# A bank of two buffers for transposed keys, and a threshold search with two serial VectorE operations a bit

## The chip, the cores and the metric

The kernel runs on one core of a Trainium2 chip. The metric is the device time of one execution in microseconds; the time of a version is the median of its runs. One execution of each version is also recorded by the hardware profiler, and that recorded execution has a time of its own.

## The reference

One inference step of a one-layer hybrid encoder for a prompt of 1,024 tokens and eight samples of 16 tokens (128 more columns, 1,152 in all). What matters here is the sparse attention's choice of keys and the gated delta rule.

```python
h = _rmsnorm(x, norm_mix)
qa, ka, va, qi, ki, wi, qb, kb, vb, gb, bb, ab, ga, gbr = jnp.split(h @ w_in, ...)
...
# mixer A: every query keeps its top-k keys by an index score, then softmax attention on those
score = jnp.einsum('bqhs,bqh->bqs', jax.nn.relu(s), wi)
score = jnp.where(adm[None], score, NEG)
_, idx = lax.top_k(score, topk)
...
# mixer B: gated delta rule; q and k are l2-normalised, then a triangular system per chunk
qh = _l2norm(qb_c) * (DK ** -0.5)
kh = _l2norm(kb_c)
a_mat = strict_lower(kb @ kc.T * decay) + eye
sol = triangular_solve(a_mat, rhs)
...
x = x + (sigmoid(ga) * (oa @ w_proj_a) + sigmoid(gbr) * (ob @ w_proj_b)) @ w_out
x = x + (gelu(conv(h2 @ w_up_gate)) * (h2 @ w_up_val)) @ w_down
```

## The kernel before

Every dense product is made in three passes: weights and activations are split into a rounded part (H, wh) and a remainder (L, wl), and TensorE adds H·wh, L·wh and H·wl for each tile of 128 rows. The columns stand in three blocks of 384; one block of one tile of `w_in` is 8·3 = 24 products into one of three PSUM banks (`acc`). These products are the filler: they run from the start of the kernel until the feed-forward network takes over, and everything else of the mixers is set between them.

The program writes no fixed order. Each piece of work is a generator, a thread with a priority; at each `yield` it names the engine that it wants next, an event, a bank, or the end of its own transfers (`DMA`). `_Driver.run` (line 165) takes the thread that by the driver's own table of costs can start first, and among equals the one with the lowest number, and lets it issue its next instructions. So the order of instructions on each engine comes out of the driver's costs, and each engine then works through its list strictly in that order. A `_Banks` object (line 47) is a set of buffers that the driver knows of: a thread that yields the bank gets a buffer only once one has been given back, by the driver's clock. A tile that is taken straight from a pool (`p.tile`) is not known to the driver: the hardware waits for its last user, but the order is written as if there were no wait.

The stage at hand begins when the scores of the indexer are there, and runs beside the dense products. Two sets of threads share it.

The choice of keys (`topk_rows`, line 294) searches, for every query, the threshold that keeps the wanted number of scores, one bit at a time. Rows 0 to 2 (thread "v", priority 8) and row 6 ("s", priority 7) count on VectorE. Rows 3 to 5 ("a", priority 7, `ACT_SUM`) count on ScalarE: for each of 31 bits VectorE makes a candidate (`cand`, line 1344), ScalarE takes the sign of each score less the candidate and sums (three `ja` instructions of 768, 896 and 1,024 elements, line 1348), and VectorE compares (line 1351), scales the bit (line 1353) and puts it into the threshold (line 1355). All the small operations work on 128 x 3 elements of the tile `cola`. After the last bit VectorE turns the thresholds into masks (lines 1393 to 1422), with operations over whole rows of scores.

The delta rule's local part (`gdn_local`, line 1430) prepares four heads, 0 to 3. `gdn_squares` (line 1612) transposes queries and keys of a head in groups of 4, 4 and 1 tiles of 128 into a PSUM bank (`gd`, five of them); for keys, ScalarE copies the bank into the tile `kt` (line 1624) and SP stores it (line 1626); then ScalarE squares the bank in place and VectorE sums it and gives the bank back. `gdn_tiles` (line 1551) makes the 128 x 128 blocks `nt` and `at`; `gdn_rows` (line 1633) solves 72 small triangles of 16 x 16 on VectorE by 15 steps of two operations (`pr` and `zs`); `gdn_inverses` and `gdn_levels` (lines 1668 and 1688) join them to inverses of 64 x 64 by products, with ScalarE copies (`lv`, `W`) between them. `gdn_v` (line 1493) transposes the values through the same PSUM banks.

Beside this `evac_conv` (line 936) filters blocks of the projection in two buffers `ext`; it stores the last columns of each (`out_cb`, lines 986 and 987) in pieces of three elements.

`mixers` (line 660) runs `gdn_local` to its end, then waits for the three sets of thresholds (line 720), and only then spawns attention and the scan of the delta rule. At the end of attention the samples' outputs are stored, loaded again, split, and taken by the products with `w_proj_a`, which follow those with `w_proj_b`.

Of the kernel before, what the change touches and what calls it, by code (L numbers as in the profile page):

```python
# [7 lines left out]
F32 = mybir.dt.float32  # L8
F32R = mybir.dt.float32r
BF = mybir.dt.bfloat16  # L10
I32 = mybir.dt.int32
# [285 lines left out]
class _Kernel:  # L297
# [996 lines left out]
    def topk_rows(self, s0, s1, ACT_SUM, z):  # L1294
# [8 lines left out]
        def col(dt=F32):  # L1303
            o = next(free)
            return cols[:, o:o + nr] if dt == F32 else cols[:, o:o + nr].bitcast(dt)
# [31 lines left out]
        if ACT_SUM:  # L1337
            cand, bit = col(I32), col(I32)
            yield DVE
            nc.vector.scalar_tensor_tensor(ka[:, s], kk[:, s], 2.0, nn[:, s], op0=OP.mult, op1=OP.add)  # L1340
            nc.vector.memset(thr[:, s], 0)
            for b in range(30, -1, -1):
                yield DVE
                nc.vector.tensor_scalar(cand[:, s], thr[:, s], (1 << b) - (1 << 31), None, op0=OP.bitwise_or)
                for i in R:
                    o, n = segs[i][:2]
                    yield ACT
                    nc.scalar.activation(ja[:, :n], SC[:, o:o + n], AF.Sign, bias=cand.bitcast(F32)[:, i:i + 1],
                                         accum_out=cnt[:, i:i + 1])
                yield DVE  # L1350
                nc.vector.tensor_tensor(acc[:, s], cnt[:, s], ka[:, s], op=OP.is_ge)
                yield DVE
                nc.vector.tensor_scalar(bit[:, s], acc[:, s], float(1 << b), None, op0=OP.mult)
                yield DVE
                nc.vector.tensor_tensor(thr[:, s], thr[:, s], bit[:, s], op=OP.bitwise_or)
        else:
# [73 lines left out]
    def gdn_local(self, st):  # L1430
# [7 lines left out]
        self.kqs = _Banks(p, [128, 2, T], "kq", 2)  # L1438
        self.vcs = _Banks(p, [128, 512], "vc", 1)
        self.nts = _Banks(p, [128, 9, 128], "nt", 1)  # L1440
        self.lvs = _Banks(p, [128, 512], "lv", 2)
# [170 lines left out]
    def gdn_squares(self, kq, ss, w, gsc):  # L1612
        nc, p = self.nc, self.gd
        for a, z in GR:
# [6 lines left out]
            if w:  # L1621
                kt = p.tile([128, 512], F32, name="kt")
                yield ACT
                nc.scalar.copy(kt[:, :n * 128], pk[:, :n * 128])
                yield SP
                nc.sync.dma_start(gsc[:, a:z, 0], v3(kt, n))
            yield ACT
            nc.scalar.activation(pk[:, :n * 128], pk[:, :n * 128], AF.Square)
# [1439 lines left out]
```

## Time and profile before

| | |
|---|---|
| runs, us | 2136.8, 2140.67, 2141.2; median 2140.67 |
| the profiled execution's own time, us | 2142.78 |
| its span, first to last instruction, us | 2140.8 |
| mean granted TensorE clock | 0.984 |
| busy: PE, weight loads, DVE, ACT, POOL | 97%, 94%, 72%, 47%, 39% |
| instructions | 37,600 |

All instructions go through one helper (line 192), so the profile is read by tile names and by time. The search of the thread "a" stands between 256.7 us and 590.1 us (first and last `ja`), the key copies `kt` between 314.0 and 477.0 us. PE is TensorE, DVE VectorE, ACT ScalarE, POOL GpSimd; SP issues the transfers. "Idle before" in square brackets is the time in which the engine stood still ahead of an instruction, with what released it.

### The profile page before, as it was taken

How to read it: one execution, taken by the hardware profiler on the slowest of the kernel's cores; microseconds unless marked ns; L12 is line 12 of the kernel's file. 1: busy time of each engine (PE TensorE's matmuls, PEld its weight loads, DVE VectorE, ACT ScalarE, POOL GpSimd, SP SyncE). 2: the span in 40 equal slices, each digit the busy share in tenths (PEclk: the TensorE clock that was granted, in tenths of full speed). 3: DMA queues.
4: the chain of work that ended last, by engine and by line, in shares of the span. 5: the costliest groups of instructions: out<-in, count | busy, mean ns of one | idle time of the engine just before them, and what ended most of it. 6: DMA issues, size and time to landing. Idle time of an engine off the chain costs nothing.

```text
span 2140.8 us, 37600 instructions
## 1 busy us (share of the span) xinstructions
PE 2068.0 (97%) x13146; PEld 2007.1 (94%) x13146; DVE 1544.1 (72%) x3588; ACT 999.3 (47%) x1979; POOL 838.4 (39%) x1024
## 2 busy tenths in 40 slices
PE   7999998989999999999999999999999999999997
PEld 6899997979999999999999989999999999999997
DVE  7268988888756778784353778878788766857656
ACT  5267666665625566666223433333333344535333
POOL 5344434432234444554364445656556500201101
PEclk8999999989999999999999999999999999999998
DMA  5444366676556555546774433433444476656542
GB/s 196 110 132 101 84 184 158 161 192 180 160 167 210 179 179 159 160 130 217 246 230 146 131 69 65 81 84 64 83 66 81 89 181 212 191 175 215 179 140 92
DMA packets 318156, 314.56 MB, mean 147 GB/s; under 512 B 117436, under 2 KB 277008, under 8 KB 317840
## 3 DMA queue, kind: packets, MB, share of 16 engines
q1 hardware_dynamic: 317968, 312.17, 53.2%
q8 instruction: 104, 1.70, 0.4%
q14 instruction: 84, 0.69, 0.1%
HBM read 224.91 MB, written 88.81 MB: 147 GB/s over the span
## 4 chain that ended last, share of the span: by engine, by line
PE 53%; DMA 7%; DVE 3%; issue 1%; POOL 1%; ACT 1%; SPq 1%; DVEq 0%; ACTq 0%; POOLq 0%
PE up L192 22%; PE dn L192 14%; PE acc L192 10%; PE at L192 6%; DMA T<-in_w_down 1%; DMA evo<-gates 1%; SPq L192 1%; DMA pbT<-evo 1%; PE rp L192 1%; DMA obT<-sg 1%; DMA ppT<-evo 1%; DVE B L192 0%; POOL tg L192 0%; DMA x<-qkv 0%; DVE wl L192 0%
## 5 line engine op out<-in xcount | busy, mean ns | idle before, releaser
L192 PE MATMUL acc<-H,wh 128*128 128x384 f32 (+2 forms) x1344 | 478.8, 356 | 10.8 <-ACT wh L192 3.1
L192 PE MATMUL acc<-H,wl 128*128 128x384 f32 (+2 forms) x1344 | 458.9, 341 | 1.6 <-POOL wl L192 1.6
L192 PE MATMUL acc<-L,wh 128*128 128x384 f32 (+2 forms) x1344 | 458.6, 341 | 1.5 <-POOL L L192 1.3
L192 POOL TENSOR_TENSOR wl<-wr,wh 128x256 fp32r<-128x256 f32 (+1 forms) x288 | 232.3, 829 | 308.8 <-ACT wh L192 301.3
L192 PEld LDWEIGHTS acc<-H,wh 128*128 128x128 f32 (+1 forms) x1344 | 255.3, 190 | 21.8 <-ACT wh L192 5.1
L192 PEld LDWEIGHTS acc<-L,wh 128*128 128x128 f32 (+1 forms) x1344 | 255.5, 190 | 6.2 <-POOL L L192 2.0
L192 PEld LDWEIGHTS acc<-H,wl 128*128 128x128 f32 (+1 forms) x1344 | 254.9, 190 | 4.3 <-POOL wl L192 2.9
L192 POOL TENSOR_TENSOR ssq<-ssq,sqs 128x384 f32<-128x384 f32 x62 | 71.8, 1158 | 390.4 <-ACT sqs L192 385.2
L192 ACT CAST wh<-wr 128x1024 fp32r<-128x1024 f32 (+3 forms) x140 | 122.7, 883 | 149.5 <-PE dn L192 48.3
L192 POOL TENSOR_TENSOR wl<-s,wh 128x256 fp32r<-128x256 f32 x104 | 98.7, 968 | 146.6 <-ACT wh L192 146.6
L192 PE MATMUL up<-B,wh 128*128 128x288 f32 x704 | 142.2, 296 | 1.0 <-DVE u L192 1.0
L192 DVE SCALAR_TENSOR_TENSOR T<-fe,cwf,T 128x512 f32<-128x512 f32 x132 | 123.4, 935 | 17.8 <-ACT T L192 16.2
L192 PEld LDWEIGHTS up<-B,wh 128*128 128x128 f32 x704 | 112.9, 188 | 1.3 <-DVE u L192 1.3
L192 ACT ACTIVATE ja<-SC,cola 128x768 bf16<-128x768 f32 (+2 forms) x93 | 96.7, 1039 | 34.5 <-DVE cola L192 25.1
L192 ACT CAST wh<-s 128x512 fp32r<-128x512 f32 x88 | 52.5, 620 | 120.3 <-PE up L192 113.4
L192 PE MATMUL up<-T,wh 128*128 128x288 f32 x352 | 104.3, 296 | 1.8 <-DVE T L192 1.8
L192 PE MATMUL up<-B,wl 128*128 128x288 f32 x352 | 104.0, 296 | 0.0
L192 DVE TENSOR_TENSOR wl<-wr,wh 128x512 fp32r<-128x512 f32 (+1 forms) x87 | 71.8, 840 | 30.3 <-ACT wh L192 30.2
L192 POOL TENSOR_TENSOR cvc<-cvc,evo 128x384 f32<-128x384 f32 (+2 forms) x48 | 44.0, 917 | 76.8 <-ACT evo L192 53.7
L192 DVE TENSOR_SCALAR_CACHE_REDUCE e<-half,colv 128x384 bf16<-128x384 int16 (+5 forms) x96 | 71.1, 740 | 0.9
L192 PEld LDWEIGHTS up<-T,wh 128*128 128x128 f32 x352 | 66.4, 189 | 2.5 <-DVE T L192 2.5
L192 PE MATMUL acc<-MH,wl 128*128 128x384 f32 x192 | 65.3, 340 | 2.7 <-POOL wl L192 2.7
(507 smaller groups left out, 6108.0 us busy)
## 6 DMA issues: line engine op xcount, KB each, us to landing
wr<-in_w_in SPq DMA_DIRECT2D x48, 512.0 KB, 3.8
AT<-fv SPq DMA_DIRECT2D x22, 576.0 KB, 6.2
wr<-in_w_down SPq DMA_DIRECT2D x24, 512.0 KB, 3.6
T<-in_w_down SPq DMA_DIRECT2D x24, 512.0 KB, 3.6
wr<-in_w_up SPq DMA_DIRECT2D x22, 512.0 KB, 11.1
gates<-evo SPq DMA_DIRECT2D x48, 192.0 KB, 2.0
T<-AT SPq DMA_DIRECT2D x44, 192.0 KB, 3.7
qkv<-evo SPq DMA_DIRECT2D x36, 192.0 KB, 4.0
```

Source lines behind the costliest of these rows:

```text
L192: r = f(*a, **k)
```

## The change

The copies of transposed keys get a bank of two buffers that the driver knows of, in place of one tile from the pool. The candidate of the search carries the sign bit and the bit under test with it: while ScalarE counts, VectorE makes `base`, the candidate with the present bit taken out and the next one set; after the count one operation compares, and one shifts the result to its bit and joins it to `base`. The final threshold is the candidate without the sign bit.

```diff
         if ACT_SUM:
-            cand, bit = col(I32), col(I32)
+            cand, base, bit = col(I32), col(I32), col(I32)
             yield DVE
             nc.vector.scalar_tensor_tensor(ka[:, s], kk[:, s], 2.0, nn[:, s], op0=OP.mult, op1=OP.add)
-            nc.vector.memset(thr[:, s], 0)
+            nc.vector.memset(cand[:, s], 0)
+            nc.vector.tensor_scalar(cand[:, s], cand[:, s], (1 << 30) - (1 << 31), None, op0=OP.bitwise_or)
             for b in range(30, -1, -1):
+
                 yield DVE
-                nc.vector.tensor_scalar(cand[:, s], thr[:, s], (1 << b) - (1 << 31), None, op0=OP.bitwise_or)
+                nc.vector.tensor_scalar(base[:, s], cand[:, s], 3 << b - 1 if b else 1, None, op0=OP.bitwise_xor)
                 for i in R:
                     o, n = segs[i][:2]
                     yield ACT
                     nc.scalar.activation(ja[:, :n], SC[:, o:o + n], AF.Sign, bias=cand.bitcast(F32)[:, i:i + 1],
                                          accum_out=cnt[:, i:i + 1])
                 yield DVE
-                nc.vector.tensor_tensor(acc[:, s], cnt[:, s], ka[:, s], op=OP.is_ge)
+                nc.vector.tensor_tensor(bit[:, s], cnt[:, s], ka[:, s], op=OP.is_ge)
                 yield DVE
-                nc.vector.tensor_scalar(bit[:, s], acc[:, s], float(1 << b), None, op0=OP.mult)
-                yield DVE
-                nc.vector.tensor_tensor(thr[:, s], thr[:, s], bit[:, s], op=OP.bitwise_or)
+                nc.vector.scalar_tensor_tensor(cand[:, s], bit[:, s], b, base[:, s],
+                                               op0=OP.logical_shift_left, op1=OP.bitwise_or)
+            yield DVE
+            nc.vector.tensor_scalar(thr[:, s], cand[:, s], (1 << 31) - 1, None, op0=OP.bitwise_and)
...
         self.vcs = _Banks(p, [128, 512], "vc", 1)
+        self.kts = _Banks(p, [128, 512], "kt", 2)
...
             if w:
-                kt = p.tile([128, 512], F32, name="kt")
+                kt = yield self.kts
                 yield ACT
                 nc.scalar.copy(kt[:, :n * 128], pk[:, :n * 128])
                 yield SP
                 nc.sync.dma_start(gsc[:, a:z, 0], v3(kt, n))
+                self.drv.give(self.kts, kt)
```

Both edits change what the driver sees, so it writes another order on every engine from the middle of the indexer on. Three places matter for what follows. In the rows a wait on DMAHW0 to DMAHW7 is a wait for a transfer: SP's transfers take these eight lanes in turn, and a transfer's own row names the lane that it takes, which its predecessor on the lane must have left.

ACT, the key copies of head 1 (`kt`), with the counts of the search (`ja`), the weights (`wh`) and the filter (`ext`, `cvc`, `evo`) around them. Before:

```order
L192 COPY kt<-gd_3801 128x512 [waits DMAHW7_49,PE_49,Activation_49]
L192 ACTIVATE gd_3812<-gd_3812 128x128 [waits PE_49]
L192 ACTIVATE gd_3801<-gd_3801 128x512
L192 ACTIVATE ja,cola<-SC,cola 128x768 [waits DVE_49]
L192 ACTIVATE ja,cola<-SC,cola 128x896 [waits Activation_49]
L192 CAST wh<-wr 128x1024 [waits DMAHW6_49]
L192 ACTIVATE cvc_3868<-ext_3849,cwb 128x384 [waits DVE_49,Pool_49]
L192 COPY kt<-gd_3847 128x128 [waits DMAHW3_49,PE_49]
L192 ACTIVATE ja,cola<-SC,cola 128x1024 [waits Activation_49]
L192 ACTIVATE evo_3869<-ext_3849,cwb 128x384
L192 ACTIVATE ext_3904<-acc_3850 128x384 [waits DMAHW5_49,DMAHW4_49,PE_49]
```

ACT at the same place, with the change:

```order
L192 COPY kt_3799<-gd_3790 128x512 [waits PE_49]
L192 ACTIVATE evo_3708<-cvc_3677 128x384 [waits DVE_49]
L192 ACTIVATE gd_3792<-gd_3792 128x128 [waits PE_49]
L192 CAST wh<-wr 128x1024 [waits DMAHW4_49]
L192 ACTIVATE gm_3783<-gm_3783,ngc 128x128 [waits Pool_49]
L192 ACTIVATE gd_3790<-gd_3790 128x512
L192 ACTIVATE ja,cola<-SC,cola 128x768
L192 ACTIVATE ja,cola<-SC,cola 128x896 [waits Activation_49]
L192 ACTIVATE ja,cola<-SC,cola 128x1024 [waits Activation_49]
L192 ACTIVATE cvc_3890<-ext_3861,cwb 128x384 [waits DVE_49,Pool_49]
L192 COPY kt_3897<-gd_3886 128x128 [waits DMAHW1_49,PE_49]
L192 ACTIVATE ext_3920<-acc_3862 128x384 [waits DMAHW7_49,DMAHW0_49,PE_49]
```

The second copy no longer waits for a transfer; the third does, for the lane of the first buffer's store. The copy into `ext` waits for the small stores `out_cb` in both.

SP, the stores around the same copies. Before:

```order
L192 DMA gsc<-vc_3172 128x4x128 [waits DMAHW3_49,DVE_49]
L192 DMA out_cb<-ext_3387 128x3 [waits DMAHW4_49]
L192 DMA out_cb<-ext_3387 128x8x3 [waits DMAHW5_49]
L192 DMA wr<-in_w_in 128x1024 [waits DMAHW6_49,Pool_49]
L192 DMA gsc<-kt 128x4x128 [waits DMAHW7_49,Activation_49]
L192 DMA qkv<-evo_3624 128x384 [waits DMAHW0_49,DVE_49]
```

SP at the same place, with the change:

```order
L192 DMA gsc<-kt_3734 128x4x128 [waits DMAHW1_49,Activation_49]
L192 DMA kTs<-evo_3749 128x384 [waits DMAHW2_49,Activation_49]
L192 DMA out_kT<-evo_3749 128x384 [waits DMAHW3_49]
L192 DMA wr<-in_w_in 128x1024 [waits DMAHW4_49,Pool_49]
L192 DMA gm_3783<-gcr 128x128 [waits DMAHW5_49,DVE_49]
L192 DMA gsc<-vc_3088 128x4x128 [waits DMAHW6_49,DVE_49]
L192 DMA out_cb<-ext_3533 128x3 [waits DMAHW7_49]
L192 DMA out_cb<-ext_3533 128x8x3 [waits DMAHW0_49]
L192 DMA gsc<-kt_3799 128x4x128 [waits DMAHW1_49,Activation_49]
```

The first key store of this head and a load of weights have moved ahead of the two `out_cb`; the second key store stands behind them.

DVE, the last third of head 3's triangles (`pr`, `zs`). Before:

```order
L192 SCALAR_TENSOR_TENSOR pr<-ns,zs 72x100 [waits DVE_49]
L192 TENSOR_REDUCE zs<-pr 72x10 [waits DVE_49]
L192 SCALAR_TENSOR_TENSOR pr<-ns,zs 72x121 [waits DVE_49]
L192 TENSOR_REDUCE zs<-pr 72x11 [waits DVE_49]
L192 SCALAR_TENSOR_TENSOR pr<-ns,zs 72x144 [waits DVE_49]
L192 TENSOR_REDUCE zs<-pr 72x12 [waits DVE_49]
```

DVE at the same place, with the change:

```order
L192 SCALAR_TENSOR_TENSOR pr<-ns,zs 72x100 [waits DVE_49]
L192 SCALAR_TENSOR_TENSOR eq_6460<-SC,cola,eq_6460 128x896
L192 TENSOR_REDUCE zs<-pr 72x10 [waits DVE_49]
L192 TENSOR_TENSOR MB<-MB,eq_6460 128x896 [waits DVE_49]
L192 SCALAR_TENSOR_TENSOR pr<-ns,zs 72x121 [waits DVE_49]
L192 TENSOR_SCALAR MB<-MB 128x896 [waits DVE_49]
L192 TENSOR_REDUCE zs<-pr 72x11 [waits DVE_49]
L192 TENSOR_SCALAR MB<-SC,cola 128x1024
L192 SCALAR_TENSOR_TENSOR pr<-ns,zs 72x144 [waits DVE_49]
L192 TENSOR_SCALAR eq_6575<-MB 128x1024 [waits DVE_49]
L192 TENSOR_SCALAR MB,cola<-MB 128x1024 [waits DVE_49]
L192 TENSOR_REDUCE zs<-pr 72x12
```

The masks of the search (`MB`, `eq`) now stand between the steps of the triangles; before they followed them.

## Rows read from the trace of the kernel before

**Rows 1.** Page, part 1: busy time of each engine over the span
```profile
PE 2068.0 (97%) x13146; PEld 2007.1 (94%) x13146; DVE 1544.1 (72%) x3588; ACT 999.3 (47%) x1979; POOL 838.4 (39%) x1024
```
**Rows 2.** Stretches of 100 us: length, busy us by engine, granted clock, DMA, GB/s
```profile
300.00:400.00 100.00, 90.86 (x511) 85.94 (x509) 84.74 (x324) 64.63 (x142) 40.64 (x63) 0.97 0.70 183
400.00:500.00 100.00, 92.88 (x530) 88.09 (x529) 85.22 (x351) 58.62 (x126) 32.25 (x47) 0.90 0.71 185
```
**Rows 3.** Timeline of ACT: start, us, instruction, idle before it
```profile
341.99 1.06 ACT L192 ACTIVATE gd<-gd 128x512 f32<-128x512 f32 x2
352.91 0.58 ACT L192 COPY kt<-gd 128x512 f32<-128x512 f32 x1 [9.86 <-DMA gsc<-kt]
...
405.42 0.27 ACT L192 COPY kt<-gd 128x128 f32<-128x128 f32 x1 [2.80 <-DMA gsc<-kt]
```
**Rows 4.** The tile kt: all waits of its engine, us and times
```profile
  DMA gsc<-kt: 12.7, 2
```
**Rows 5.** Timeline of SP's issues around the wait
```profile
341.35 1.05 SPq L192 DMA_DIRECT2D out_cb<-ext  x2
342.50 0.61 SPq L192 DMA_DIRECT2D wr<-in_w_in  x1
343.21 0.38 SPq L192 DMA_DIRECT2D gsc<-kt  x1
```
**Rows 6.** The tensor out_cb: its 24 small stores, issue to landing
```profile
DMA to landing us min/median/max: 6.2/7.0/7.7
```
**Rows 7.** Timeline of DVE, the first operation after the wait
```profile
353.69 0.29 DVE L192 TENSOR_REDUCE ss<-gd 128x1 f32<-128x128 f32 x1 [6.81 <-ACT gd L192]
```
**Rows 8.** Timeline of PE: around the wait, and at 450 us
```profile
355.56 1.09 PE L192 MATMUL gd<-c,vc 128*128 128x128 f32 x4 [4.21 <-DVE at L192]
...
449.78 2.61 PE L192 MATMUL gd<-Z,lv 128*128 128x64 f32 x11 [1.07 <-ACT lv L192]
```
**Rows 9.** Three shorter stretches, columns as in rows 2
```profile
355.00:365.00 10.00, 9.44 (x41) 9.29 (x42) 9.96 (x36) 7.92 (x21) 6.57 (x12) 0.71 0.39 118
...
390.00:430.00 40.00, 40.00 (x230) 39.22 (x229) 33.90 (x138) 21.68 (x49) 14.72 (x25) 1.00 0.63 147
...
445.00:475.00 30.00, 25.08 (x158) 22.00 (x157) 22.70 (x93) 19.67 (x43) 9.98 (x13) 0.72 0.59 167
```
**Rows 10.** Timeline of PE: two products of an unbroken run of 15
```profile
299.71 0.34 PE L192 MATMUL acc<-L,wh 128*128 128x384 f32 x1
...
302.14 0.34 PE L192 MATMUL acc<-H,wh 128*128 128x384 f32 x1
```
**Rows 11.** Timeline of DVE: the four serial operations of a late bit
```profile
584.18 0.16 DVE L192 TENSOR_TENSOR cola<-cola 128x3 f32<-128x3 f32 x1
584.38 0.17 DVE L192 TENSOR_SCALAR cola<-cola 128x3 int32<-128x3 f32 x1
584.58 0.16 DVE L192 TENSOR_TENSOR cola<-cola 128x3 int32<-128x3 int32 x1
584.78 0.17 DVE L192 TENSOR_SCALAR cola<-cola 128x3 int32<-128x3 int32 x1
```
**Rows 12.** The tile cola on DVE: the one two-step operation of 128 x 3
```profile
L192 DVE SCALAR_TENSOR_TENSOR cola<-cola x1: 151/151/151, 254.1 to 254.1; 128x3 f32<-128x3 f32 x1
```
**Rows 13.** Timeline of ACT at 446 us: a late count and the copy behind it
```profile
446.00 0.93 ACT L192 ACTIVATE ja<-SC,cola 128x768 bf16<-128x768 f32 x1 [2.79 <-DVE cola L192]
...
449.38 0.62 ACT L192 COPY lv<-gd 128x256 f32<-128x256 f32 x2
```
**Rows 14.** Timeline of DVE: head 3's last triangle step, first and last masks
```profile
578.47 0.38 DVE L192 TENSOR_REDUCE zs<-pr 72x15 f32<-72x225 f32 x1
...
595.12 0.68 DVE L192 TENSOR_SCALAR MB<-SC,cola 128x768 bf16<-128x768 f32 x1
...
621.60 1.11 DVE L192 TENSOR_TENSOR MB<-MB,eq 128x1024 bf16<-128x1024 bf16 x1
```
**Rows 15.** Timeline of PE: the last products of attention
```profile
1018.82 1.05 PE L192 MATMUL at<-szn,svN 128*128 128x128 f32 x8
```
**Rows 16.** Timeline of POOL: the last piece of attention's output is split
```profile
1033.97 1.02 POOL L192 TENSOR_TENSOR L<-L,H 128x384 fp32r<-128x384 f32 x1 [2.80 <-ACT H L192]
```

## The prediction

> **What bounds the kernel now.** I read the busy shares first: TensorE is busy for 2068.0 of 2140.8 us [rows 1]. Nothing that another engine does can move the end unless it moves TensorE's work, its idle time, or its clock. The change adds and removes no product, so only the 73 us of idle time and the stretches at a lower clock are to be had. Stretch by stretch, the part in which the changed code runs holds more of both than the parts around it: 9.14 us of idle time between 300 and 400 us and 7.12 us between 400 and 500, with the granted clock at 0.97 and 0.90 [rows 2]. These 200 us are where the key copies and most of the search stand.
>
> The waits of the tile kt come next. ScalarE stood still for a key store twice, 12.7 us in all [rows 4]: 9.86 us ahead of the copy at 352.91, and 2.80 us ahead of the one at 405.42 [rows 3]. The first can be followed to TensorE. The store of the first buffer was issued at 343.21, behind two small stores issued from 341.35 [rows 5], which take 6.2 to 7.7 us to land [rows 6]. ScalarE's list is strictly in order, so the squares that stand behind the copy came late, VectorE's sums waited 6.81 us for them [rows 7], the PSUM banks came free late, and TensorE stood still for 4.21 us until 355.56 [rows 8]. It then came back at half speed: the mean granted clock from 355 to 365 us is 0.71 [rows 9], a mixture of 1.2 and 2.4 GHz. The second wait cost nothing: from 390 to 430 us TensorE was busy throughout [rows 9].
>
> **The key copies.** They stay twelve, with twelve stores, of the same size; the bank adds only memory. In the new order of head 1 the second copy waits for TensorE alone. The third waits for the first buffer's store, which now stands ahead of the two small stores, not behind them. So the 9.86 us go, and with them TensorE's 4.21 us. The clock goes with the gap: 9.44 busy us at 0.71 are 9.44 x 0.29 = 2.7 us lost. The bounds are nothing, if another wait takes the place, and 4.2 + 2.7 = 6.9. I take 6.9, because the row is this very wait and the order shows it gone. What is late next on ScalarE is the copy into the filter's buffer (ext), three instructions behind a count: it waits for the small stores, as before.
>
> **The search.** For each of 31 bits four serial operations become two, and one more (base) runs while ScalarE counts. Undisturbed, the steps of a bit are 0.20 us apart (584.18, 584.38, 584.58, 584.78) [rows 11], so two fewer save 0.4 us, and the search 31 x 0.4 = 12.4 us. Where VectorE is full the steps are further apart: of the 2.79 us that ScalarE waited for a candidate at 446.00 [rows 13] part was this. One operation joins two steps, a shift and an or; the only row for such an operation on 128 x 3 has 0.151 us, and the single-step ones 0.16 and 0.17 [rows 12, 11], so it costs no more. What is this worth on TensorE? Between 0 and the idle time that I can tie to a late candidate: at 449.38 ScalarE made a copy that stood behind three counts [rows 13], and TensorE had waited 1.07 us for it [rows 8]. I take that 1.1 and put the rest at nothing, since the cover is plain: while the search goes on TensorE has dense products to do, and these don't depend on it. If that cover went (no dense products left before the mixers end), the 12.4 us would count in full.
>
> Nor does the search alone open the next stage. Attention waits for the masks and for the delta rule's local part. Before, head 3's last triangle was done at 578.47 and the masks came after it, from 595.12 to 621.60 [rows 14]. In the new order these masks stand between the triangle's steps on VectorE, so head 3 is finished later, not earlier. Counting the dense products that stand ahead of attention's first product in TensorE's list gives 2,580 before and 2,694 now. An unbroken run of them has 14 steps from 299.71 to 302.14, 0.174 us each [rows 10], so attention is some 20 us of dense work later. That costs nothing by itself: 114 products done before need not be done after.
>
> **The sum.** 4.2 + 2.7 + 1.1 = 8.0 us. The profiled execution took 2142.8 us, so its like would be 2134.8; the median of the runs, 2140.67, stands 2.1 us lower. From the median the forecast is **2132.7 us**, 0.37% less.
>
> One rule speaks for a larger sum. The rows 300 to 500 us show TensorE idle for 9.14 + 7.12 = 16.3 us by its products, and for 14.06 + 11.91 = 26.0 us by its weight loads [rows 2]. The Trainium skill (Perfetto Trace Analysis, "Identifying the Most-Contended Engine") holds the products' busy share to be a poor measure and the weight loads' the good one. By it the most that the stretch can give would be 26.0 us instead of 16.3 before any clock; I go by the products, because my terms are single gaps between them.
>
> **Rivals.**
> First, **the wait only moves**. The copy into ext waits for the small stores themselves, and a second buffer doesn't change that. Between the second key copy and that copy the new list holds ScalarE work that I add up to some 7 us from like rows, against 6.2 to 7.7 us of landing [rows 6]; a microsecond or two of wait fits, 9.86 does not, unless SP issues late. The whole order is rewritten too, and such a collision can fall on another place. Then the 6.9 us stay and only 1.1 us go: 2139.6 us, no change. The key store issued at 343.21 freed ScalarE only at 352.9, after the small stores ahead of it [rows 3, 5]. The Trainium skill (DMA: Bandwidth & Descriptors, "Queues, rings and completion order") says that a transfer's signal lands only after all earlier writes of the same DMA engine. The trace agrees; by that rule every wait for a transfer issued behind an out_cb stays as long as it was.
>
> Second, **the pile after 445 us goes as well**. There head 0's levels meet head 3's keys and late counts of the search: 30.00 - 25.08 = 4.9 us idle, and 25.08 x 0.28 = 7.0 us of clock [rows 9], 11.9 in all, of which 1.1 is in my sum. If ScalarE, rid of late candidates, serves these levels in time, another 10.8 us go: 2121.9 us. Against it: the same pieces stand together in the new order, and the counts are packed closer.
>
> Third, on the other side, **the later attention runs into the products that need it**. By TensorE's list attention ended 282 dense products ahead of the first product with w_proj_a; now it is 99. From the last product of attention at 1018.82 [rows 15] the samples' outputs are stored, loaded and split until 1034.99 [rows 16]: 16.2 us. The new list leaves 99 products and 18 more ahead of the third block, 117 x 0.174 = 20.4 us. It fits by 4 us. If the store and the loads, which now meet the loads of gates and weights, took twice as long, 32.4 us, TensorE would stand still for 12.0 us and lose 2.7 us of clock after it: 2132.7 + 14.7 = 2147.4 us. The point from which it decides is a chain of some 26 us: 20.4, and the 5.3 that with 2.7 of clock eat up the 8.0 gained.
>
> **The numbers.** Forecast 0.50, for its mechanism is one row long and the order shows the wait gone; the wait moves 0.25; the pile goes too 0.10; late attention 0.15. A measurement of this kernel can tell about 0.2%, 4.3 us, from no change. Faster is then 0.50 + 0.10 = 0.60, same 0.25, slower 0.15. The range has to reach the second rival's 2121.9 below and, for what of the third is short of its price, nearly 2147.4 above: 2121 to 2146. The forecast's own range is 2127 to 2136, from half of the key term on the one side to half of the pile on the other.
>
> **What would show it.** Right: no wait of ScalarE for gsc<-kt above 3 us; no gap of TensorE near 4 us while heads 0 to 2 are prepared; idle time between 300 and 500 us near 11 us in place of 16.3; the search's last count some 12 us earlier, near 578 us; the masks among head 3's triangles, and attention's first product later than before. Wrong: a wait of ScalarE for out_cb of 5 us or more, with the same gap behind it; a clock as low as 0.90 between 400 and 500 us with new gaps ahead of it; or TensorE idle for over 5 us at the first products with w_proj_a.

## The result, and the profile after

The changed kernel takes 2125.01 us, the median of four runs (2120.38 to 2129.47), beside 2138.76 us for the kernel before (four runs, 2136.8 to 2141.2). The ratio is 0.9934, with a 95% interval of 0.9914 to 0.9955. The time lies in the range of 2121 to 2146 us and on the side that was forecast, but the gain is 13.7 us where 8.0 were worked out. The profiled execution took 2129.47 us, its span 2127.7.

The page of the changed kernel, part 1, stands against [rows 1]:

```profile
PE 2058.5 (97%) x13146; PEld 2000.3 (94%) x13146; DVE 1532.1 (72%) x3556; ACT 1003.4 (47%) x1984; POOL 838.4 (39%) x1022
```

Its stretches, with the columns of [rows 2]; the third answers to the last of [rows 9]:

```profile
300.00:400.00 100.00, 96.95 (x560) 94.50 (x559) 91.22 (x365) 75.11 (x161) 42.15 (x64) 0.98 0.74 191
400.00:500.00 100.00, 97.99 (x610) 94.11 (x609) 92.58 (x365) 68.91 (x144) 35.76 (x51) 0.97 0.81 188
445.00:475.00 30.00, 30.00 (x203) 27.72 (x202) 27.26 (x93) 20.75 (x48) 10.22 (x13) 0.91 0.90 176
...
900.00:1000.00 100.00, 95.55 (x604) 91.88 (x603) 66.85 (x201) 65.89 (x156) 51.21 (x78) 0.95 0.65 203
```

The gain comes out of the 200 us that the prediction named. TensorE's idle time there fell from 16.3 us to 3.05 + 2.01 = 5.1. What the clock takes (busy time times what the granted clock lacks to 1) fell from 90.86 x 0.03 + 92.88 x 0.10 = 12.0 us to 96.95 x 0.02 + 97.99 x 0.03 = 4.9. From 445 to 475 us there is no idle time in place of 4.9 us. That stretch no longer holds the whole pile, though: the first product of the levels (`gd<-Z,lv`) starts at 439.0 us in place of 449.8. From 430 to 475 us 2.0 us of idle time are left of 7.1 (the rows stand under e). A part is given back between 900 and 1000 us, where attention now stands: 4.45 us idle, against 2.11 before, at a clock of 0.95 in place of 1.00.

TensorE's waits from 300 to 500 us (engine and tile, what it waited for, us in total, times, longest):

```profile
PE gd L192 <- DMA vc<-qkv: 2.0, 1, 2.0
PE gd L192 <- ACT lv L192: 1.2, 1, 1.2
PE acc L192 <- ACT ext L192: 1.0, 1, 1.0
```

The largest is for a load of values (`vc`), which before was none of its waits. ScalarE's two waits for key stores [rows 3, 4] are gone; what is left of its waits in the same range, 230 to 700 us, for `kt` and for the small stores:

```profile
ACT kt L192 <- PE gd L192: 2.1, 2, 1.5
ACT ext L192 <- DMA out_cb<-ext: 1.4, 2, 0.9
```

The search ends 43 us earlier. First the counts on ScalarE (first and last start in us; before, the last was at 589.0), then two steps of a late bit on VectorE, with work on masks (`MB`) between them:

```profile
L192 ACT ACTIVATE ja<-SC,cola x93: 915/1042/1153, 261.4 to 546.2; 128x768 bf16<-128x768 f32 x31, 128x896 bf16<-128x896 f32 x31, 128x1024 bf16<-128x1024 f32 x31
```

```profile
543.10 0.15 DVE L192 TENSOR_TENSOR cola<-cola 128x3 int32<-128x3 f32 x1
543.22 0.29 DVE L192 TENSOR_SCALAR MB<-MB 128x512 bf16<-128x512 bf16 x1
543.43 0.16 DVE L192 SCALAR_TENSOR_TENSOR cola<-cola 128x3 int32<-128x3 int32 x1
...
587.21 0.38 DVE L192 TENSOR_REDUCE zs<-pr 72x15 f32<-72x225 f32 x1
```

The joined operation takes 0.16 us, as was taken from [rows 11, 12]. Head 3's last triangle step starts at 587.21, 8.7 us later than in [rows 14], and attention's last products start later too, against 1018.82 in [rows 15]:

```profile
1043.74 1.05 PE L192 MATMUL at<-szn,svN 128*128 128x128 f32 x8
```

### The profile page after: what moved, and what is told of

Its sections match the earlier page's. It is cut to its first block, busy times and chain, and to the rows that moved or that the text cites. A ratio compares the mean times of both kernels' runs of the same rounds, so it can differ in the third digit from the quotient of the medians.

```text
span 2127.7 us, 37559 instructions
## 1 busy us (share of the span) xinstructions
PE 2058.5 (97%) x13146; PEld 2000.3 (94%) x13146; DVE 1532.1 (72%) x3556; ACT 1003.4 (47%) x1984; POOL 838.4 (39%) x1022
## 4 chain that ended last, share of the span: by engine, by line
PE 79%; DVE 8%; DMA 6%; ACT 2%; issue 2%; POOL 2%; SPq 1%; DVEq 0%; POOLq 0%; ACTq 0%
PE acc L192 29%; PE up L192 22%; PE dn L192 15%; PE at L192 7%; PE gd L192 2%; PE ix L192 1%; DVE e L192 1%; SPq L192 1%; DMA qr<-qiT 1%; POOL wl L192 1%; PE ac L192 1%; DMA wr<-in_w_in 1%; PE rp L192 1%; DMA T<-in_w_down 1%; DVE B L192 1%
## 5 line engine op out<-in xcount | busy, mean ns | idle before, releaser
L192 ACT ACTIVATE z<-z,mx 128x896 f32<-128x896 f32 (+7 forms) x83 | 63.2, 766 | 20.1 <-DVE mx L192 19.7
```

What stands on the lines that cost most here:

```text
L192: r = f(*a, **k)
```

## The experiments

Three things changed together: a second key buffer, two serial operations in place of four, and the lists that the driver writes. The runs take them apart. They ran in three groups, each on a chip of its own with the kernel before beside it: a to d (median of the kernel before 2134.6 us), e, g, n1 and m1 (2135.0 us), and the rest (2132.7 us). So across groups only ratios and gains are compared, not times. The ratio stands as recorded, with its interval; it can differ from that of the two medians by some 0.001 (n2: 0.9960 and 0.9972). "Idle" is TensorE's from 300 to 500 us, "clock" what the granted clock takes there (as above, but from one row for the whole 200 us, whose clock is rounded to 0.01, some 2 us), both from the one profiled execution; "last count" is the last start of `ja`. "Changed" is the execution of the section above.

| run | lists | operations a bit | key buffers | median, us | ratio to before (95%) | idle, us | clock, us | last count, us |
|---|---|---|---|---|---|---|---|---|
| before | before's | 4 | 1 | | 1 | 16.3 | 12.9 | 589.0 |
| a | before's | 4 | 2 | 2132.22 | 0.9990 (0.9973 to 1.0006) | 13.6 | 9.3 | 583.3 |
| b | before's | 2 | 1 | 2131.81 | 0.9989 (0.9974 to 1.0005) | 14.2 | 9.3 | 581.4 |
| e | before's | 2 | 2 | 2128.99 | 0.9975 (0.9959 to 0.9991) | 12.6 | 5.6 | 575.8 |
| g | changed | 4 | 2 | 2130.44 | 0.9980 (0.9970 to 0.9991) | 9.0 | 3.8 | 547.9 |
| d | changed | 2 | 1 | 2124.52 | 0.9958 (0.9943 to 0.9973) | 10.6 | 0.0 | 545.2 |
| changed | changed | 2 | 2 | 2125.01 | 0.9934 (0.9914 to 0.9955) | 5.1 | 5.8 | 546.2 |
| after again | changed | 2 | 2 | 2120.34 | 0.9933 (0.9916 to 0.9950) | 4.1 | 2.0 | 537.5 |
| c | own, old work and bank | 4 | 2 | 2137.38 | 1.0019 (1.0005 to 1.0033) | 14.0 | 7.4 | 587.3 |
| n1 | own, old work | 4 | 1 | 2151.20 | 1.0075 (1.0053 to 1.0097) | 28.5 | 17.2 | 613.2 |
| n2 | own, old work | 4 | 1 | 2126.73 | 0.9960 (0.9944 to 0.9976) | 15.5 | 12.9 | 590.4 |
| h | own, one yield a bit | 4 | 1 | 2135.28 | 1.0010 (0.9996 to 1.0023) | 16.0 | 11.0 | 520.9 |
| m1 | own, new work | 2 | 2 | 2121.82 | 0.9940 (0.9920 to 0.9959) | 11.1 | 1.9 | 551.2 |
| p | own, new work, packed stores | 2 | 2 | 2118.59 | 0.9926 (0.9911 to 0.9941) | 7.6 | 5.8 | 561.6 |

### a: the second buffer alone, every list as before

```diff
-                kt = p.tile([128, 512], F32, name="kt")
+                kt = p.tile([128, 512], F32, name="kt", bufs=2)
```

> Only the second buffer: the tile kt gets two buffers in its pool, of which the planning driver knows nothing, so every instruction of every engine stands in the order of before. Theory 1 (the key store's wait held TensorE): ScalarE's 9.86 us wait ahead of the second key copy of head 1 is gone, TensorE's 4.2 us gap near 355 us and the half clock after it go with it, about 6.9 us less than before, near 2132 us. Rival A (the rewritten order gave the gain): the wait only moves to the copy into ext, 0 to 3 us less. Rival B (the shorter search gave the gain): as rival A.

The wait for the key store is gone (12.7 us before [rows 4], 0.4 now), and yet the ratio is 0.9990, not told from 1. The gap stayed at its place. TensorE's timeline, SP's issues ahead of it, and the stretch that answers to the first of [rows 9]:

```profile
354.26 0.63 PE L192 MATMUL gd<-c,vc 128*128 128x128 f32 x4 [3.33 <-DMA vc<-qkv]
```

```profile
341.28 1.06 SPq L192 DMA_DIRECT2D out_cb<-ext  x2
342.44 0.57 SPq L192 DMA_DIRECT2D wr<-in_w_in  x1
343.11 0.38 SPq L192 DMA_DIRECT2D gsc<-kt  x1
343.58 0.46 SPq L192 DMA_DIRECT2D qkv<-evo  x1
344.13 0.64 SPq L192 DMA_DIRECT2D gm<-gcr  x1
344.87 0.40 SPq L192 DMA_DIRECT2D vc<-qkv  x1
```

```profile
355.00:365.00 10.00, 10.00 (x50) 9.82 (x49) 6.64 (x34) 5.51 (x14) 5.45 (x9) 0.83 0.78 223
```

Before, TensorE stood still for 4.21 us ahead of the very same product, the first with this load of `vc`, and the trace put it down to VectorE [rows 8]. With that out of the way it stands still for 3.33 us, for the load of the values, which was issued 3.6 us behind the two small stores `out_cb`; the clock after it is 0.83 in place of 0.71. ScalarE, too, has a new wait there: 3.10 us at 350.92, for the load of weights (`wr`) issued at 342.44. The transfers of 340 to 350 us, rate in 40 slices of 0.25 us:

```profile
GB/s 289 362 363 375 369 350 246 205 291 289 249 34 18 18 122 16 0 16 16 0 16 0 0 16 16 33 262 82 16 49 33 49 33 98 82 98 82 16 334 285
DMA packets 2265, 1.31 MB, mean 131 GB/s; under 512 B 1249, under 2 KB 2159, under 8 KB 2265
```

From 342.75 to 349.5 us the rate is 0 to 122 GB/s but for one slice of 262, with 205 to 375 ahead of it and 285 to 334 behind it; 1,249 of the packets are under 512 bytes, and the two `out_cb` alone have 1,152 pieces. So the first rival's mechanism was at work: what is issued behind the small stores comes late, and whoever waits for it waits on. The Trainium skill (DMA: Bandwidth & Descriptors, "Specifications") names 512 bytes as the least transfer for full rate; the pieces of `out_cb` have 12. The trace agrees, as far as it goes: the rate is low while they are under way. No run here tries pieces near 512 bytes.

### b: the short search alone, every list as before

```diff
-                nc.vector.tensor_scalar(cand[:, s], thr[:, s], (1 << b) - (1 << 31), None, op0=OP.bitwise_or)
+                raw.tensor_scalar(base[:, s], cand[:, s], 3 << b - 1 if b else 1, None, op0=OP.bitwise_xor)
+                note(DVE, 0.08)
...
-                nc.vector.tensor_scalar(bit[:, s], acc[:, s], float(1 << b), None, op0=OP.mult)
+                raw.scalar_tensor_tensor(cand[:, s], bit[:, s], b, base[:, s],
+                                         op0=OP.logical_shift_left, op1=OP.bitwise_or)
+                note(DVE, 0.08)
                 yield DVE
-                nc.vector.tensor_tensor(thr[:, s], thr[:, s], bit[:, s], op=OP.bitwise_or)
+                note(DVE, 0.08, True)
```

> Only the search with two serial operations a bit, in the order of before: the driver is told of the four old operations at their old places, so what is left out is one VectorE operation a bit and two steps of each candidate's chain. One key buffer. Theory 1: 0 to 2 us less than before (the 1.1 us of the copy that stood behind three counts), near 2138 us; ScalarE's 25.1 us of waiting for candidates falls by half or more. Rival A: no change within 2 us. Rival B: 8 us less or more, 2131 us or below.

Here `raw` issues an operation that the driver does not see, and `note` tells it the cost of one that is not issued. 0.9989, and again not told from 1. The waits for key stores stay (12.9 us), TensorE waits 2.56 us at 353.76 for the same load of values. ScalarE's waits for candidates (`cola`) fell from 25.1 us to 10.9, as expected, and the time hardly moved. The gap of 1.07 us that the prediction tied to a late candidate is gone, but the wait just ahead of it, for a load (`W`), grew from 0.91 to 2.30 us. In before's lists each edit measures some 2 us, and by the intervals at most some 6.

### e: both edits, every list as before

The edits of a and b together.

> Both edits in the hardware, the second buffer and the two serial operations, but every engine keeps the list of before: the driver is told of the old four operations and of no bank. If the edits act by themselves (theory 1, the forecast's terms), their parts add up: TensorE's 4.2 us gap of before at 355 us and the lower clock go, and late candidates no longer hold ScalarE, 2132.7 us by the forecast's sum, a ratio near 0.996. If the two edits alone hide under each other's waits (each alone gave 0.999), the ratio is 0.998 to 0.999, 2130 to 2133 us on this chip's scale of 2134.6. If the gain of the change needs the new list (theory 2), this stays 7 us or more above the 2124 to 2125 us of the changed kernel.

0.9975: within the intervals the two parts add up, 2135.0 x 0.0025 = 5.3 us, in place of 8.0. The wait for the values is still there, 3.69 us at 351.42. The changed kernel's interval (0.9916 to 0.9950, third group) does not touch this one, so the lists carry some of the gain. One place where they do is the largest gap of the pile after 445 us. Before, TensorE waited 2.43 us there for a copy `lv`; ScalarE's rows between its two copies (some left out) hold no count and no wait:

```profile
457.58 0.73 ACT L192 COPY lv<-gd 32x256 f32<-32x256 f32 x2
458.34 1.05 ACT L192 CAST wh<-wr 128x1024 fp32r<-128x1024 f32 x1
...
461.50 0.73 ACT L192 COPY lv<-gd 32x256 f32<-32x256 f32 x2
```

```profile
462.28 0.68 PE L192 MATMUL gd<-Z,lv 128*64 128x64 f32 x8 [2.43 <-ACT lv L192]
```

It is the order of ScalarE's list that makes this gap: it is 2.43 us in a, b and e as well. In the changed kernel's list the four copies of this step stand together:

```profile
445.89 1.50 ACT L192 COPY lv<-gd 32x256 f32<-32x256 f32 x4
```

There the gap is gone in the changed kernel's first profile, 0.24 us in its second and 0.92 us in d and g (below). The stretch from 430 to 475 us, which holds the pile in all of them: of the kernel before, of e, of g with its four operations in the changed lists, and of the changed kernel:

```profile
430.00:475.00 45.00, 37.88 (x219) 34.09 (x218) 37.60 (x152) 29.71 (x63) 15.66 (x21) 0.77 0.71 195
```

```profile
430.00:475.00 45.00, 39.86 (x269) 37.30 (x268) 41.38 (x172) 29.11 (x64) 14.50 (x18) 0.92 0.80 208
```

```profile
430.00:475.00 45.00, 42.21 (x297) 39.34 (x296) 42.56 (x178) 33.34 (x73) 13.90 (x19) 1.00 0.80 182
```

```profile
430.00:475.00 45.00, 42.99 (x287) 39.84 (x286) 42.19 (x166) 30.33 (x69) 12.73 (x16) 0.92 0.81 173
```

### c and d: one edit with its own lists

c has the three lines on the bank of the change and the old search; d has the new search and one buffer from the pool, and its lists are the changed kernel's, row for row.

> The change without its search: a bank of two key buffers that the driver knows of, the old search of four operations. The driver writes an order of its own. Theory 1: no wait of ScalarE for a key store above 3 us, about 7 us less than before, near 2132 us, give or take what the other order does. Rival A: anything between 2124 and 2147 us, with no relation to the waits of kt. Rival B: no change, within 3 us of before.

> The change without its bank: the short search as changed, one key buffer from the pool. Its order of instructions is that of the changed kernel, row for row, so against the changed kernel it differs only by the waits on the one buffer. Theory 1: the third copies, whose predecessor's store stands behind the small stores out_cb, wait up to 8 us in head 1; 3 to 7 us slower than the changed kernel, 2128 to 2132 us, and only 7 to 11 us faster than before. Rival A: within 3 us of the changed kernel, near 2126 us. Rival B: as rival A.

The bank with the lists that the driver then writes makes nothing faster (1.0019). The new search with its lists gives 0.9958 without a second buffer. What the buffer is worth there shows in d's ScalarE and TensorE timelines:

```profile
465.26 0.27 ACT L192 COPY kt<-gd 128x128 f32<-128x128 f32 x1 [9.27 <-DMA gsc<-kt]
```

```profile
467.10 0.45 PE L192 MATMUL acc<-H,wh 128*128 128x384 f32 x1 [1.63 <-ACT evo L192]
474.95 0.44 PE L192 MATMUL acc<-H,wh 128*128 128x384 f32 x1 [1.69 <-ACT wh L192]
```

The stretch from 450 to 500 us, first of d, then of the changed kernel's second profile ("after again"):

```profile
450.00:500.00 50.00, 44.73 (x262) 42.58 (x260) 41.14 (x159) 29.59 (x58) 14.82 (x21) 1.00 0.72 172
```

```profile
450.00:500.00 50.00, 49.41 (x302) 47.66 (x300) 47.23 (x189) 33.66 (x68) 16.99 (x24) 1.00 0.78 196
```

With one buffer the last key copy waits 9.27 us, and TensorE is idle for 5.3 us there in place of 0.6. The ratios differ by about as much, 0.0025 x 2133 = 5.3 us, but the gains by the medians only by 2.3 us (10.1 and 12.4), and the intervals overlap (0.9943 to 0.9973 and 0.9916 to 0.9950). By the trace the buffer pays, at 465 us in the new lists, not at 353 in the old; the times make that likely and do not show it.

### g: four operations in the changed kernel's lists; and the changed kernel again

```diff
-                nc.vector.tensor_scalar(base[:, s], cand[:, s], 3 << b - 1 if b else 1, None, op0=OP.bitwise_xor)
+                raw.tensor_scalar(cand[:, s], thr[:, s], (1 << b) - (1 << 31), None, op0=OP.bitwise_or)
+                told("tensor_scalar", base[:, s], cand[:, s])
...
-                nc.vector.scalar_tensor_tensor(cand[:, s], bit[:, s], b, base[:, s],
-                                               op0=OP.logical_shift_left, op1=OP.bitwise_or)
+                raw.tensor_scalar(bit[:, s], acc[:, s], float(1 << b), None, op0=OP.mult)
+                raw.tensor_tensor(thr[:, s], thr[:, s], bit[:, s], op=OP.bitwise_or)
+                told("scalar_tensor_tensor", cand[:, s], bit[:, s], b, base[:, s])
```

> The lists of the changed kernel on TensorE, ScalarE, GpSimd and SP, row for row, with two key buffers, but the old search in them: four serial operations a bit, and the driver is told of the new ones. With the runs before it this fills the square of old and new lists by four and two operations. If the lists alone make the gain (theory 2a: the order is what counts), the ratio stays at 0.995 to 0.996 and the time at 2124 to 2126 us. If the shorter chain of a bit is needed in that order (theory 2b), the last count comes some 10 us later than the 546 us of the changed kernel, ScalarE waits for cola well over the 13 us seen there, and the time goes back by half of the gain or more, to 2129 us or above.

> The changed kernel unchanged, beside the others of this call and the kernel before on the same chip. By its first runs it stands at a ratio of 0.9934. With one key buffer and the same lists the ratio was 0.9958; if the second buffer is worth what it seems (theory 1 in part, some 4 us in the new lists), this one stays at 0.9935 or below; if it is worth nothing there (theory 2), the two agree within their intervals, at 0.995 to 0.996, 2124 to 2126 us.

In g `told` gives the driver the cost of the operation that the changed kernel has at this place. g gives 0.9980 and closes a square, all with two buffers: old lists and four operations 0.9990 (a), old lists and two 0.9975 (e), new lists and four 0.9980 (g), new lists and two 0.9933. No interval of the first three touches the last one's, so neither the lists nor the short search is enough alone. (By adding the two steps one would have 0.9965, above the last interval, but these steps have intervals of their own: whether the pair gives more than its parts is not settled.) The last count was expected some 10 us later than 546.2 and came at 547.9. So most of the 43 us is made by the lists, not by the operations; a share of some 10 us can't be told, since the changed kernel's own two profiles have 546.2 and 537.5. In before's lists the two operations alone bring it forward by some 7.5 us (589.0 to 581.4 from before to b, 583.3 to 575.8 from a to e). What the two operations cost in the new lists shows in ScalarE's waits ahead of the counts, first g's, then the changed kernel's in the second profile, and in one gap of g's TensorE:

```profile
ACT ja L192 <- DVE cola L1347: 23.8, 14, 4.3
```

```profile
ACT ja L192 <- DVE cola L192: 12.9, 8, 2.8
```

```profile
496.44 3.48 PE L192 MATMUL gd<-Z,lv 128*128 128x64 f32 x16 [1.77 <-ACT lv L192]
```

At 492.43 g's ScalarE had stood still 3.63 us for a candidate; its copy `lv`, three counts further down, started at 496.03, and TensorE waited for it. A candidate that is late holds, through ScalarE's list, copies that have nothing to do with the search. This gap is not all of g's loss: its largest, 2.77 us at 321.99 (0.99 in the changed kernel), stands behind a ScalarE operation that waited for VectorE's filter sum (`cvc`), not for a candidate.

### n1, n2 and m1: other lists for the same work

```diff
-    LAT, MARGIN = 0.2, 0.2
+    LAT, MARGIN = 0.21, 0.2
```

This is n1 on the kernel before and m1 on the changed one; n2 has `0.2, 0.21` on the kernel before. The work is the same, the driver only reckons with other costs and so writes other lists.

> The kernel before, with the same work, but the driver's latency between engines set to 0.21 us in place of 0.20, so that it writes other lists (1,672 rows of TensorE's list differ, about as many as between the two kernels). If the gain of the change is the luck of a rewritten list (theory 2c), a rewritten list of the old work should spread as widely: 2125 to 2145 us, ratio anywhere from 0.995 to 1.005. If the new search is what makes the better list (theory 2d), this stays with the old family, 2132 to 2138 us, ratio 0.999 to 1.002.

> The changed kernel, with the same work, but the driver's latency set to 0.21 us, so that it writes other lists (1,826 rows of TensorE's list differ from the changed kernel's). If the gain is the luck of one list (theory 2c), it is as likely lost as kept: 2125 to 2138 us. If the driver writes a better list because the search takes less of VectorE's and ScalarE's time by its costs (theory 2d), the gain stays: 2122 to 2128 us, ratio 0.994 to 0.997, with the last count of the search some 40 us ahead of that of the kernel before with the same latency.

> The kernel before with the same work, but the driver's margin for TensorE set to 0.21 us in place of 0.20: another list of the old work (1,368 rows of TensorE's list differ from before's). The first rewritten list of the old work took 16 us more than before, the first of the new work 3 us less than the changed kernel. If old work makes lists of 2134 us and above and that loss was one bad collision, this gives 2132 to 2140 us, last count of the search at 575 us or later. If luck decides, this is as likely to reach the new family's 2122 to 2126 us as not.

The old work's lists spread from 0.9960 (n2) to 1.0075 (n1). In n1 one gap alone takes 12 us, ahead of a product of the delta rule; the trace puts it down to VectorE's counts (`colv`, another of the searches):

```profile
491.62 0.77 PE L192 MATMUL gd<-kq 128*128 128x256 f32 x1 [12.03 <-DVE colv L192]
```

n2's profiled execution took 2134.49 us, the top of its runs, and m1's 2130.64, 9 us above its median, so their traces say little of their medians. The three lists for the new work in two buffers (changed, m1, p) give 0.9926 to 0.9940, the five for the old search (before, c, n1, n2, h) 0.9960 to 1.0075. So a list's luck is worth as much as was forecast for the whole change. That luck alone set the two groups apart is unlikely, but not excluded: the medians don't mix, while n2's interval (0.9944 to 0.9976) overlaps those of the new work; with the same latency of 0.21 us the new work is 29 us faster than the old. How much of the 0.9933 is this list's own luck stays open with so few lists.

### h: four operations behind one yield

```diff
+            yield DVE
             for b in range(30, -1, -1):
-                yield DVE
                 nc.vector.tensor_scalar(cand[:, s], thr[:, s], (1 << b) - (1 << 31), None, op0=OP.bitwise_or)
...
-                yield DVE
                 nc.vector.tensor_scalar(bit[:, s], acc[:, s], float(1 << b), None, op0=OP.mult)
-                yield DVE
                 nc.vector.tensor_tensor(thr[:, s], thr[:, s], bit[:, s], op=OP.bitwise_or)
```

> The kernel before with one key buffer and the old four serial operations a bit, but written behind one yield in place of four, so that no other thread's work can be set between them on VectorE; the driver writes its own list (1,668 rows of TensorE's list differ from before's, 740 from the changed kernel's). If what the change shortens is the number of places at which a bit queues for a VectorE that is 85 to 90% busy (theory 3), the last count comes by 550 us or sooner with the operations uncut, as in the changed kernel (546.2), and the time falls by half of the change's gain or more: 2123 to 2129 us, ratio 0.994 to 0.998. If the operations themselves are what counts (the forecast's 0.4 us a bit), the last count stays near 589 us less nothing, and the time near the old family's 2133 to 2137 us. If the list is luck alone, the last count may be early and the time anywhere from 2122 to 2151 us.

Half of it came. The last count starts at 520.9 us, 68 us before that of the kernel before, with no operation cut: a bit's length is set by how often it queues for VectorE (the old search with its four yields ends at 587.3 to 613.2 us in before, c, n1 and n2). But the time is 1.0010, so an early end of the search is worth nothing by itself. Counts that follow each other fill ScalarE's list, and other copies come late. h's ScalarE (rows between left out) and TensorE:

```profile
427.37 0.94 ACT L192 ACTIVATE ja<-SC,cola 128x768 bf16<-128x768 f32 x1 [0.65 <-DVE cols L192]
...
428.59 1.03 ACT L192 ACTIVATE ja<-SC,cola 128x896 bf16<-128x896 f32 x1
...
429.61 1.03 ACT L192 CAST wh<-wr 128x1024 fp32r<-128x1024 f32 x1
```

```profile
430.70 0.48 PE L192 MATMUL acc<-H,wh 128*128 128x384 f32 x1 [4.07 <-ACT wh L192]
```

The rounded weights (`wh`) are made behind two counts, and TensorE's dense products, the filler itself, wait 4.07 us for them. That this is what ate the early end is read from these rows, not tried by itself.

### p: the changed kernel with packed output columns

```diff
+                co = self.cvp.tile([128, 27], F32, name="co", bufs=2)
+                yield POOL
+                nc.gpsimd.tensor_copy(co[:, 0:3], ext[:, 256:259])
+                nc.gpsimd.tensor_copy(co[:, 3:27].rearrange("p (b q) -> p b q", q=3), es[:, :, 16:19])
                 yield SP
-                nc.sync.dma_start(O["cb"][ch][:, 0:3], ext[:, 256:259])
-                nc.sync.dma_start(O["cb"][ch][:, 3:27].rearrange("p (b q) -> p b q", q=3), es[:, :, 16:19])
+                nc.sync.dma_start(O["cb"][ch][:, 0:27], co)
```

> The changed kernel with the 27 output columns of each filter block first put together on GpSimd (two copies of 128x3 and 128x8x3 into one tile) and stored in 128 pieces of 108 bytes in place of 1,152 pieces of 12 bytes; the lists are rewritten by that too (1,082 rows of TensorE's differ). Both kernels' small stores take 6 to 8 us to land and hold what stands behind them. If that landing still costs TensorE something (waits of ScalarE for out_cb, late loads of values), the landing falls to 2 to 3 us, those waits go, and the time falls below the changed kernel's by 2 to 4 us: 2120 to 2123 us. If nothing on the path waits for it any more, the time is the changed kernel's within the spread of a rewritten list, 2121 to 2129 us.

The landing of `out_cb`, which in the changed kernel is no shorter than in [rows 6], and then in p:

```profile
DMA to landing us min/median/max: 7.0/7.7/8.4
```

```profile
DMA to landing us min/median/max: 1.4/3.3/3.4
```

TensorE's wait for `vc` from 300 to 500 us and ScalarE's for `out_cb` are gone. The time is 2118.59 us beside 2120.34, ratios 0.9926 and 0.9933 with intervals that lie within each other for the most part: the lowest median of all, but no gain over the changed kernel that is shown. In its place stands one wait of 3.8 us for `wh`, in lists that were again written anew.

## Why the prediction came out as it did

**The place was right, the main term was not.** Idle time and clock were to be had between 300 and 500 us, and there the gain lies. 97% of the span is TensorE's before and after. But of the 8.0 us of the sum 6.9 were to come from a gap that the buffer alone left in place, and the gain of 13.7 us came in good part from what the sum left out: the order of the new lists. That the time fell on the forecast's side and into the range is to that extent luck; it lies below the forecast's own range of 2127 to 2136.

**The key copies, 6.9 us: the step failed.** It said that the 9.86 us of wait go "and with them TensorE's 4.21 us". The wait went, the gap did not (a: 3.33 us, ratio 0.9990). I followed the chain back to one releaser and did not ask who else would be late at the same product. The second buffer seems to pay 2 to 5 us all the same, by a wait of 9.27 us in the new lists that the view of before could not show. The first rival named the right cause, the small stores, and the wrong victim: ScalarE's copy into `ext` waits for `out_cb` only 1.4 us, the load of `vc` is what comes late.

**The search, 1.1 us: mis-sized, and its cover misjudged.** It was priced at 1.1 us from one gap. It measured two to three microseconds in the old lists (b; and e beside a), and 2133 x (0.9980 - 0.9933) = 10 us in the new ones (8 by the medians' gains). I put the rest at nothing "since the cover is plain": dense products don't depend on the search. But ScalarE serves both, strictly in order, and a late candidate (g) or a count that stands first (h) holds the copies that TensorE waits for.

**The last count, 12 us earlier: 43 and 51 us.** The 0.4 us a bit is the undisturbed length, and in the old lists the operations alone gave some 7.5 us. The rest is the lists'. VectorE is over 90% busy in the changed kernel from 300 to 500 us, and each step fewer is a queue fewer in the list (g, h). It is no gain by itself (h).

**The second rival named the right place,** and 0.10 was too little for it. Most of the pile went: from 430 to 475 us 7.1 us of idle time fell to 2.0, the clock rose from 0.77 to 0.92 (and 1.1 us and 0.96 in the second profile). In size the gain of 13.7 us (12.4 by the medians of the second pair) stands about midway between the forecast's 8.0 and the rival's 18.8. Its reason, that ScalarE is rid of late candidates, is not what did it: in e the candidates' chain is short and 5.1 us of that idle time stay, in g it is long and only 2.8 stay. The largest gap that the lists differ in, 2.43 us, holds no candidate: what differs is where ScalarE's copies stand. What spoke against the rival, that the same pieces stand together, did not matter: they were served in time.

**Late attention did not come.** Attention's last products did start 25 us later (16 in the second profile), but TensorE's longest gap from 700 to 1300 us is 1.94 us, at 1097.49, and that is for a weight's remainder (`wl`), not for attention's output. What later attention costs, at most, is idle time from 900 to 1000 us: 4.45 us, where before 97.89 of these 100 us were busy.

**The signs.** Of those named as right, no wait for a key store above 3 us and the masks among the triangles came. Attention stands behind more dense products, but by the clock its first product on the prompt's keys (`kH`) started at 670.86 us in the one profile and 662.21 in the other, against 667.97 before: later in one, earlier in the other. Idle time near 11 us was too cautious (5.1 and 4.1). A gap near 4 us in heads 0 to 2 did not come, but one of 1.65 to 1.96 us for `vc` did.

## What to carry to other kernels

When a wait is taken out, look for the next thing that the same instruction needs, and above all for what was issued behind the same slow transfer: in a, 9.86 us of wait went and 0.9 us of gap. Where a planner writes the order, hold the order and run the edit alone, and rewrite the order with the work unchanged: here the edits gave 0.25% in the old order, and orders of the same work differ by more than 1%. A short dependent step on a nearly full engine can cost its place in the queue more than its duration (h), and an engine that works through its list in order passes the delay on to work that has nothing to do with it (g).

## What the runs showed of the hardware

Two stores of 128 and 1,024 pieces of 12 bytes, 13.5 KB in all, keep the transfers slow for some 6.75 us (342.75 to 349.5 in a), to 122 GB/s and less but for one slice, where 200 to 375 flow on either side; in 128 pieces of 108 bytes the same columns land in 3.3 us. In the kernel before the rate behind them falls in the same way, to 0 to 147 GB/s from 343.0 to 349.75 us. Removing that from the changed kernel (p) moved the time by nothing that could be told from no change; p's lists were written anew as well, so what the packing is worth by itself stays open.
